# A two-layer decoder trunk: six experts fetched ahead and eleven groups instead of four and ten, and the second residual added by VectorE

## The chip, the cores and the metric

The kernel runs on one core of one Trainium2 chip. The metric is the device time of one execution in microseconds (us), as the median of three runs. TensorE (PE) multiplies matrices into the accumulation memory PSUM, VectorE (DVE) and ScalarE (ACT) do elementwise work, GpSimd (POOL) does a few small things, and SyncE (SP) issues nearly every DMA. Each engine works through its own instructions in program order and waits on semaphores for the others.

## The reference, cut to what matters

There are 256 tokens of width 1024 and two layers. A layer first mixes tokens (two kinds of attention, gated and projected), adds the residual and normalizes. Its second half is the part that the change touches:

```python
ffn = hierarchical_moe(x, ...)     # top-1 of 4 groups, then top-2 of 8 experts in that group: 32 experts of 1024 -> 256 -> 1024
ple = jax.nn.sigmoid(x @ w_ple_gate[i]) * (p[i] @ w_ple[i])
x = layer_norm(ALPHA * x + ffn + ple, ln2_g[i], ln2_b[i])
```

Each expert has 3 MB of f32 weights. All 32 are read in every layer, since all of them may be chosen by some token.

## The kernel before, in words

**Memory.** An arena of 47 places, each 128 partitions x 1024 f32 (512 KB), holds every weight tile and most long-lived tensors (class `Held`). A load takes the place that was freed longest ago and cannot start before the last reader of that place is done. All weight loads go through SP's queue in program order, so a load that waits for its place holds up those behind it.

**Experts.** Each expert has six weight tiles of one place: four (j = 0 to 3) for the gate and up projections and two (j = 4, 5) for the down projection. Experts are worked in groups that fill the 128 slots of a tile: two experts with 64 slots each, or four with 32. `groups` lists them: `npair` groups of two, the rest of four; `order` permutes them. The first `NFIX` experts are fixed by number, so that their loads need no routing result; the others are ranked by how many tokens chose them, the `NBIG` first ranks get 64 slots, and their ids are read by SP (`value_load`, L1034) when routing is done.

**The loop over groups** (`for gi in range(len(groups))`, PE in the written order): `front(gi + 1)` multiplies the gathered tokens of the next group with its j = 0 to 3 tiles in 32 strips of 32 slots, four strips side by side on the array; `back(gi)` does the down projection of the present group; then come the gathering of tokens for group gi + 2, the transposition of the hidden tile, `combine` (eight matmuls that add the group's output to the four accumulators `ya`), and the slot weights (`ways_of`). `front` frees its places as it goes, `back` its own at its end. At gi = 3 a branch (`leftover`) is tested, whose body is for an overfull expert.

**The input embedding** (class `Embed`, four quarters of 256 columns, two token tiles each): `products` multiplies into PSUM, `gate` takes the sigmoid (ACT) and the product (DVE) and splits it into a rounded part (ACT) and a rest (DVE), and `add` brings both into `ya` by two matmuls with the identity. Quarter 0 runs at gi = e1 = 2, the quarters 1 to 3 at the gi in `early`. In layer 0 the second token tile of quarter 3 runs after the loop.

**What stands ahead of the loop in SP's order:** the loads of the fixed experts, then of the embedding's quarters 1 to `nemb`, then (layer 0 only) `ahead`, four tiles of the next layer's first projection, which the loop splits at the gi in `pre_if`.

**The residual.** After the first norm, PE writes ALPHA * x into the accumulators with four f32 matmuls against a scaled identity (`residual`, tile `hT` in the trace): one ahead of the routing product of token tile 0, three behind that of token tile 1, while DVE works out the routing.

Of the kernel before, what the change touches and what calls it, by code (L numbers as in the profile page):

```python
# [11 lines left out]
F32 = mybir.dt.float32  # L12
# [5 lines left out]
OP = mybir.AluOpType  # L18
# [5 lines left out]
DEPTH = 2  # L24
P = 128
# [16 lines left out]
FAR = 1000.0  # L42


NFIX = 4
NBIG = 8


SEC = ["iq", "sq", "sk", "sv", "dq", "dk", "dv", "ga0", "ga1", "gb0", "gb1"]
# [30 lines left out]

@with_exitstack
def tile_hybrid_trunk(ctx: ExitStack, tc: tile.TileContext, x_in, xT_in, pT_in, pos_in, ws, wik, wrt, lnv,
                      brt, lamv, sublnv, out, places=47, t2b=4, young=4, gsb=1, hTb=1, silb=2, nring=5, early=(3, 4, 5), nahead=4, apart=8, npre=36, wA=1, wB=1, wC=1, wD=1, wE=3, inorder=2, e0=2, e1=2,  nearly_=0, peng_=1, ifat=3, im=0, df=0, dh=15, nol=0, diag=1, rpool='0000', lastemb=1, lastat=5, pre_if=(6,7), npair=4, fh=False, fg=0, order=(0,1,2,4,3,5,6,7,8,9), engs=None, nemb=3, nwarm=9, nfine=2, nah=4, o1=False, o2=False, o3=True, o4=True, order2=True, pa=2, pb=7, f1=True):
    nc = tc.nc
    V, A, G = nc.vector, nc.scalar, nc.gpsimd

# [40 lines left out]
    def wt(shape, dt, tag, bufs):  # L127
        return wk.tile(shape, dt, tag=tag, bufs=bufs, name=nm(tag))
# [33 lines left out]
    def load(l, i, shape):  # L162
        r = Held(shape, load=True)
        nc.sync.dma_start(r.t, ws[l, i])
        return r
# [19 lines left out]
    def t2(shape, dt=F32):  # L185
        return wt(shape, dt, "t2", t2b)
# [266 lines left out]
    for l in range(DEPTH):  # L453
# [278 lines left out]
        class Embed:  # L732
# [26 lines left out]
            def gate(self, t):  # L759
                b = self.b  # L760
                g = wt([P, 256], F32, "sil", silb)
                A.activation(g, b[:, :256], AF.Sigmoid)  # L762
                V.tensor_tensor(g, g, b[:, 256:], op=OP.mult)  # L763
                e = t2([P, 2, 256], F32R)
                split(e[:, 0, :], e[:, 1, :], g)
                self.e[t] = e
# [11 lines left out]
        xtT = [Held([4, S]) for _ in range(2)]  # L778
        logits = bank()
        ya = [[acc() for _ in range(2)] for _ in range(TT)]  # L780
        alphai = wt([P, 2 * P], F32, "hT", hTb)[:, :P]
        V.tensor_scalar(alphai, ident, ALPHA, None, op0=OP.mult)
        emb = {0: Embed(0)}

        def turn(t, h):
# [5 lines left out]
        def route(t, some=range(KT)):  # L791
            for k in some:
                PE.matmul(logits[:, t * 36:(t + 1) * 36], xtT[k // 4].v[:, k % 4, t * P:(t + 1) * P], wr36.v[:, k, :],
                          start=k == 0, stop=k == KT - 1)

        def residual(t, h):
            PE.matmul(ya[t][h], alphai, x[t].v[:, h * 512:(h + 1) * 512], start=True, stop=False)

        def normed(t, h):


            if t == 0:
                turn(t, h)
            elif h == 0:
                for f in (lambda: residual(0, 0), lambda: route(0), lambda: emb[0].products(0, range(0, wA)),
                          lambda: turn(1, 0)):
                    with in_turn():
                        f()
            else:
                for f in (lambda: emb[0].products(0, range(wA, wB)), lambda: turn(1, 1), lambda: route(1, range(4)),  # L810
                          lambda: emb[0].products(0, range(wB, wC)), lambda: route(1, range(4, KT)),
                          lambda: residual(0, 1), lambda: residual(1, 0), lambda: residual(1, 1)):
                    with in_turn():
                        f()
                if wD > wC:
                    with in_turn():
                        emb[0].products(0, range(wC, wD))
# [247 lines left out]
            split(*y, yp)  # L1065
            return y

        def combine(y, sT, h, t, stop=False):

            PE.matmul(ya[t][h], sT[:, t, :], y[0], start=False, stop=False)  # L1070
            PE.matmul(ya[t][h], sT[:, t, :], y[1], start=False, stop=stop)


# [41 lines left out]
                        fetch(r, j)  # L1115
        for q in range(1, 1 + nemb):
            emb[q] = Embed(q)
        if l < DEPTH - 1:
            ahead.extend(load(l + 1, i, [2, 512]) for i in range(KT // 2))

        def strips(gi):

# [80 lines left out]
        for gi in range(len(groups)):  # L1203
            if gi == ifat:
                most = nc.values_load(cmi[0:1, 0:1], min_val=0, max_val=S)
            here = lambda: tc.manual_schedule(engines={mybir.EngineType.PE})
            with here():
                after = front(gi + 1, *slots) if gi < last else None
            if gi == ifat:
                leftover(most)  # L1210
            with here():
                ys = back(gi, hT)
                if gi + 2 <= last:
                    marks, slots = marks_of(gi + 2), Gathered(gi + 2 >= fg)
                    for k4 in range(2):
                        gather(marks, slots.half[k4], k4)
                units = embeds(gi)
                for e, t, some in units[:1]:
                    e.products(t, some)
                if gi < last:  # L1220
                    hT = turned(after[0], wt([P, 2 * P], F32, "hT", hTb))
                    for h in range(2):
                        for t in range(TT):
                            combine(ys[h], sT, h, t)
                    sT = after[1]
                for e, t, _ in units[:1]:
                    e.gate(t)
                for e, t, some in units[1:]:
                    e.products(t, some)
                    e.gate(t)  # L1230
                if gi + 2 <= last:
                    slots = slots, *ways_of(gi + 2, marks)
                for e, t, _ in units:
                    e.add(t)
            if l < DEPTH - 1 and gi in pre_if:
                for r in ahead[:2] if gi == pre_if[0] else ahead[2:]:
                    ready.extend(parts(r.v[:, k, :]) for k in range(2))
                    r.free()
            if gi == last - 1:
                lng, lnb = wide(2, l), wide(3, l)  # L1240
                xn = [Held([D]) for _ in range(TT)]
                if l < DEPTH - 1:
                    xT = Split(KT)
# [12 lines left out]
        for t in range(TT):  # L1256
            if t == 1 and l < DEPTH - 1 and lastemb < 2:
                with behind(ends[0] if f1 else None):
                    emb[3].gate(1)
                emb[3].add(1)  # L1260
            for h in range(2):
                combine(ys[h], sT, h, t, True)
            if t == 0 and l < DEPTH - 1 and lastemb < 2:
                emb[3].products(1)
            with behind((ysplit[1] if o3 else None) if t == 0 else (copied[1] if order2 else None)):
                power = norm.stats(t)
            ends.append(power)
            ends[t:] = [norm.apply(t, o2)]
            powers.append(power)
# [70 lines left out]
```

## Time and profile before

| | us |
|---|---|
| median of three runs | 930.41 (929.46 to 930.71) |
| the profiled execution | 927.54 |
| its span, first to last instruction | 925.7 |
| PE busy in it | 890.5 (96%) |
| DVE, ACT busy | 423.5 (46%), 341.6 (37%) |
| DMA | 280.82 MB, mean 303 GB/s |

Positions below are us from the start of the span. The loop over expert groups runs from about 228 to 457 in layer 0 and from about 687 to 912 in layer 1. A busy PE in this profile includes matmuls that are slow to follow each other, so that 96% doesn't say that PE ends every wait: the starts of successive steps have to be compared.

### The profile page before, as it was taken

Reading aid. Unit: us, or ns where it says so; the run is one execution under the profiler, and the core shown is the slowest. Engines: PE = TensorE matmul, PEld = TensorE weight load, DVE = VectorE, ACT = ScalarE, POOL = GpSimd, SP = SyncE. Lnnn points to the kernel's source line nnn. Section 1 sums busy time; section 2 is a strip of 40 time slices with the busy share of each in tenths; the row PEclk is TensorE's granted clock in tenths of the full one; section 3 lists DMA queues with packets and bytes.
Section 4 is the critical chain, followed back from the end, with each engine's and each line's share of the span. In section 5 each row is a group of like instructions: output and inputs, shape, how many; then the busy total and the mean of one; then the engine's idle time right before and its main releaser. Section 6 shows DMA issues by size and latency. Waiting matters only on the chain. (4 is left out here: it accounts for less than half of the span.)

```text
span 925.7 us, 15402 instructions
## 1 busy us (share of the span) xinstructions
PE 890.5 (96%) x5473; PEld 588.0 (64%) x5473; DVE 423.5 (46%) x1064; ACT 341.6 (37%) x692; POOL 22.2 (2%) x29
## 2 busy tenths in 40 slices
PE   8999999999999999999999999999999998999994
PEld 5877677886466556543388777778865565556531
DVE  6797566776221121222368965677742211221214
ACT  6567677641121111221146565866321121111210
POOL 0000100000000000000100000000000000000010
PEclk9999999999999999999999999999999999999998
DMA  8995143866999999999998222448649999999993
GB/s 293 414 408 196 54 131 120 290 232 244 354 379 387 416 371 419 416 417 416 416 416 347 79 92 79 133 137 282 227 176 415 413 401 416 352 416 416 416 417 132
DMA packets 79011, 280.82 MB, mean 303 GB/s; under 512 B 9160, under 2 KB 9928, under 8 KB 78928
## 3 DMA queue, kind: packets, MB, share of 16 engines
q1 hardware_dynamic: 78784, 279.78, 78.3%
q8 instruction: 44, 0.72, 0.3%
q14 instruction: 39, 0.32, 0.1%
q10 hardware_dynamic: 144, 0.00, 0.0%
HBM read 278.70 MB, written 1.05 MB: 302 GB/s over the span
## 5 line engine op out<-in xcount | busy, mean ns | idle before, releaser
L92 PE MATMUL acc<-a,a 128*128 128x512 f32 x1440 | 352.0, 398 | 2.0 <-ACT a L208 1.2
L92 PEld LDWEIGHTS acc<-a,a 128*128 128x128 f32 x1440 | 265.5, 188 | 64.7 <-DVE a L209 3.2
L92 PE MATMUL mm<-a,a 128*32 128x512 f32 (+5 forms) x1648 | 229.2, 521 | 1.2 <-DMA a<-ws 1.1
L209 DVE TENSOR_TENSOR a<-a,a 128x512 fp32r<-128x512 f32 (+1 forms) x247 | 164.8, 688 | 50.8 <-ACT a L208 49.9
L208 ACT ACTIVATE a<-a 128x512 fp32r<-128x512 f32 (+1 forms) x247 | 151.1, 631 | 99.3 <-PE acc L92 69.7
L92 PEld LDWEIGHTS mm<-a,a 128*32 128x32 f32 (+3 forms) x1648 | 107.4, 132 | 96.9 <-issue 78.0
L92 PE MATMUL mm<-a,hT 128*32 128x512 f32 x640 | 102.9, 594 | 10.1 <-DMA a<-ws 5.3
L92 PEld LDWEIGHTS mm<-gs,a 128*128 128x128 f32 x640 | 73.1, 192 | 15.5 <-PE mm L92 10.9
L92 PE MATMUL mm<-gs,a 128*128 128x128 f32 x640 | 77.0, 278 | 0.0
L92 PEld LDWEIGHTS mm<-a,hT 128*32 128x32 f32 x640 | 24.2, 110 | 80.9 <-issue 48.0
L1051 DVE SCALAR_TENSOR_TENSOR sil<-sil,wsl,mm 128x256 f32<-128x256 f32 x20 | 9.6, 481 | 127.2 <-ACT sil L1050 127.0
L1050 ACT ACTIVATE sil<-mm 128x256 f32<-128x256 f32 x20 | 7.7, 384 | 160.8 <-PE mm L92 145.5
L209 DVE TENSOR_TENSOR t<-mm,t 128x512 fp32r<-128x512 f32 x40 | 27.6, 691 | 76.6 <-ACT t L208 76.6
L208 ACT ACTIVATE t<-mm 128x512 fp32r<-128x512 f32 x40 | 23.9, 597 | 86.5 <-PE mm L92 86.4
L919 DVE CAST sT<-mm 128x256 fp32r<-128x256 f32 x20 | 8.5, 425 | 84.7 <-PE mm L92 84.7
L92 PE MATMUL acc<-t,sT 128*128 128x512 f32 x160 | 43.8, 410 | 0.0
L906 ACT ACTIVATE a<-mm 128x512 f32<-128x512 f32 x36 | 21.5, 597 | 43.1 <-PE mm L92 41.7
L92 PEld LDWEIGHTS acc<-t,sT 128*128 128x128 f32 x160 | 28.3, 189 | 7.4 <-issue 1.7
L763 DVE TENSOR_TENSOR sil<-sil,mm 128x256 f32<-128x256 f32 x16 | 6.7, 417 | 54.4 <-ACT sil L762 54.4
L762 ACT ACTIVATE sil<-mm 128x256 f32<-128x256 f32 x16 | 6.1, 384 | 67.3 <-PE mm L92 67.3
L548 ACT ACTIVATE t<-mm,mx 128x128 f32<-128x128 f32 (+1 forms) x64 | 26.0, 421 | 11.5 <-DVE mx L545 11.5
L95 PE MATMUL mm<-identr,t 128*128 128x128 f32 (+1 forms) x132 | 21.8, 278 | 4.3 <-DVE t L581 4.3
(196 smaller groups left out, 614.6 us busy)
## 6 DMA issues: line engine op xcount, KB each, us to landing
a<-ws SPq DMA_DIRECT2D x523, 512.0 KB, 9.1
a<-x_in SPq DMA_DIRECT2D x2, 512.0 KB, 9.4
out<-a SPq DMA_DIRECT2D x4, 256.0 KB, 2.7
a<-xT_in SPq DMA_DIRECT2D x3, 256.0 KB, 6.7
a<-wik SPq DMA_DIRECT2D x2, 288.0 KB, 9.1
a<-ws SPq DMA_DIRECT2D x2, 256.0 KB, 3.0
pT<-pT_in SPq DMA_DIRECT2D x2, 256.0 KB
a<-wrt SPq DMA_DIRECT2D x2, 144.0 KB
```

The costliest lines, as they stand in the source:

```text
L92: self.last = nc.tensor.matmul(*a, **k)
L95: self.last = nc.tensor.transpose(*a, **k)
L208: copied[0] = A.activation(hi, src, AF.Copy)
L209: copied[1] = eng.tensor_tensor(lo, src, hi, op=OP.subtract)
L548: A.activation(e[:, i * nk:(i + 1) * nk], b[:, i * nk:(i + 1) * nk], AF.Exp, bias=mx[:, i:i + 1], accum_out=sums[i])
L762: A.activation(g, b[:, :256], AF.Sigmoid)
L763: V.tensor_tensor(g, g, b[:, 256:], op=OP.mult)
L906: A.activation(xg, b.rearrange("p (k s) -> p k s", k=4), AF.Copy)
L919: V.tensor_copy(sT, b[:, :2 * P].rearrange("p (t q) -> p t q", t=TT))
L1050: A.activation(sil, gu[:, :FE], AF.Sigmoid)
L1051: V.scalar_tensor_tensor(sil, sil, wsl, gu[:, :FE], op0=OP.mult, op1=OP.mult)
```

## The change

Four constants of the plan move (the signature line is left out of the diff): `NFIX` 4 to 6, `NBIG` 8 to 12, `npair` 4 to 6, so that there are six groups of two and five of four, eleven in all, in the order (0,1,2,6,3,7,4,8,5,9,10). Of the embedding, quarter 1 alone is loaded ahead (`nemb` 3 to 1); `early` goes from (3,4,5) to (4,5,6), `lastat` from 5 to 6, `pre_if` from (6,7) to (7,8). The `ahead` loads move into the loop, to gi = 5. The residual's matmuls and the scaled identity go; instead DVE adds ALPHA * x to the gated embedding, and the first group's `combine` starts the accumulation.

```diff
-NFIX = 4
-NBIG = 8
+NFIX = 6
+NBIG = 12
...
                 V.tensor_tensor(g, g, b[:, 256:], op=OP.mult)
+                V.scalar_tensor_tensor(g, x[t].v[:, self.q * 256:(self.q + 1) * 256], ALPHA, g, op0=OP.mult, op1=OP.add)
                 e = t2([P, 2, 256], F32R)
...
-        alphai = wt([P, 2 * P], F32, "hT", hTb)[:, :P]
-        V.tensor_scalar(alphai, ident, ALPHA, None, op0=OP.mult)
...
-        def residual(t, h):
-            PE.matmul(ya[t][h], alphai, x[t].v[:, h * 512:(h + 1) * 512], start=True, stop=False)
...
-        if l < DEPTH - 1:
-            ahead.extend(load(l + 1, i, [2, 512]) for i in range(KT // 2))
...
-                            combine(ys[h], sT, h, t)
+                            combine(ys[h], sT, h, t, start=gi == 0)
...
+            if l < DEPTH - 1 and gi == pre_if[0] - 2:
+                ahead.extend(load(l + 1, i, [2, 512]) for i in range(KT // 2))
```

**SP, layer 0, the end of what is issued ahead of the routing result.** L164 is a load of the embedding or of the next layer, L1040 (after: L1035) one of an expert, TENSOR_LOAD of `ids` the first read of a ranked expert's number. Before:

```order
L164 DMA a_452_2295<-ws 128x1024
L164 DMA a_453_2297<-ws 128x1024
L164 DMA a_454_2299<-ws 128x1024
L164 DMA a_455_2301<-ws 128x1024
L164 DMA a_456_2303<-ws 128x1024
L164 DMA a_457_2305<-ws 128x1024
L1034 TENSOR_LOAD ids_420_2224
```

After:

```order
L1035 DMA a_452_2291<-ws 128x1024
L1035 DMA a_453_2293<-ws 128x1024
L1035 DMA a_454_2295<-ws 128x1024
L1035 DMA a_455_2297<-ws 128x1024
L1035 DMA a_456_2299<-ws 128x1024
L164 DMA a_459_2305<-ws 128x1024
L1029 TENSOR_LOAD ids_419_2218
```

Expert tiles stand where tiles of the embedding and of the next layer stood.

**PE, layer 0, from the routing product of token tile 1 to the first matmul on the routing mask.** `hT` is the scaled identity, the 128x36 rows are the routing product. Before:

```order
L92 MATMUL mm_393_2071<-a_361_1901,a_392_2070 128x36 x4
L92 MATMUL acc_395_2073<-a_277_1487,hT_398_2076 128x512
L92 MATMUL acc_396_2074<-a_278_1488,hT_398_2076 128x512
L92 MATMUL acc_397_2075<-a_278_1488,hT_398_2076 128x512
L92 LDWEIGHTS onesb_111
```

After:

```order
L95 MATMUL mm_408_2135<-identr_108,a_278_1488 128x128 x4
L92 MATMUL mm_393_2071<-a_361_1901,a_391_2069 128x36 x4
L92 MATMUL mm_393_2071<-a_361_1901,a_392_2070 128x36 x4
L92 LDWEIGHTS onesb_111
L92 MATMUL mm_412_2173<-t2_409_2149,onesb_111 32x32
```

Nothing is left on PE between the routing product and the mask.

**PE, layer 0, where the second unit of an embedding quarter is added** (`acc<-t2,identr`), among the strips of the next group's front. Before:

```order
L92 MATMUL mm_644_3332<-a_628_3273,a_614_3177 32x512
L92 MATMUL acc_396_2074<-t2_624_3242,identr_108 128x256 x2
L92 MATMUL mm_644_3332<-a_629_3284,a_614_3177 32x512
L92 MATMUL mm_644_3332<-a_630_3295,a_614_3177 32x512
L92 MATMUL mm_644_3332<-a_631_3306,a_614_3177 32x512
```

After:

```order
L92 MATMUL mm_663_3451<-a_655_3426,a_641_3330 32x512
L92 MATMUL acc_396_2074<-t2_651_3397,identr_108 128x256
L92 MATMUL mm_663_3451<-a_655_3426,a_641_3330 32x512
L92 MATMUL mm_663_3451<-a_656_3437,a_641_3330 32x512 x2
L92 MATMUL mm_663_3451<-a_657_3439,a_641_3330 32x512
L92 MATMUL acc_396_2074<-t2_651_3397,identr_108 128x256
```

Five strips stand ahead of the first add in both; the second add now follows four strips later.

## Rows read from the trace of the kernel before

**Rows 1.** PE in order of time, a back of layer 1: start, busy us, line, operation.
```profile
727.57 3.62 PE L92 MATMUL mm<-a,hT 128*32 128x512 f32 x32
```

**Rows 2.** ACT in order of time, layer 1: the sigmoid that follows each front.
```profile
856.17 0.38 ACT L1050 ACTIVATE sil<-mm 128x256 f32<-128x256 f32 x1 [7.68 <-PE mm L92]
872.99 0.39 ACT L1050 ACTIVATE sil<-mm 128x256 f32<-128x256 f32 x1 [8.88 <-PE mm L92]
890.66 0.38 ACT L1050 ACTIVATE sil<-mm 128x256 f32<-128x256 f32 x1 [9.70 <-PE mm L92]
```

**Rows 3.** PE in order of time, the last two backs of layer 1.
```profile
890.05 1.02 PE L92 MATMUL mm<-a,hT 128*32 128x512 f32 x2
...
901.48 0.44 PE L95 MATMUL mm<-identr,sil 128*128 128x128 f32 x2
...
903.86 1.65 PE L92 MATMUL mm<-a,hT 128*32 128x512 f32 x8
...
909.41 2.76 PE L92 MATMUL mm<-a,hT 128*32 128x512 f32 x18 [0.17 <-DMA a<-ws]
912.10 2.22 PE L92 MATMUL acc<-t,sT 128*128 128x512 f32 x8
```

**Rows 4.** ACT in order of time, layer 0: the sigmoids of the last two fronts.
```profile
407.21 0.39 ACT L1050 ACTIVATE sil<-mm 128x256 f32<-128x256 f32 x1 [8.88 <-PE mm L92]
...
436.13 0.38 ACT L1050 ACTIVATE sil<-mm 128x256 f32<-128x256 f32 x1 [14.69 <-PE mm L92]
```

**Rows 5.** PE in order of time, the last two backs of layer 0.
```profile
435.52 2.20 PE L92 MATMUL mm<-a,hT 128*32 128x512 f32 x4
...
446.81 0.44 PE L95 MATMUL mm<-identr,sil 128*128 128x128 f32 x2
...
449.18 1.06 PE L92 MATMUL mm<-a,hT 128*32 128x512 f32 x8
...
456.94 0.73 PE L92 MATMUL acc<-t,sT 128*128 128x512 f32 x2
```

**Rows 6.** Windows: start:end, length, busy us (count) of PE, PEld, DVE, ACT, POOL, PEclk, DMA share, GB/s.
```profile
225.00:230.00 5.00, 4.84 (x42) 3.04 (x45) 3.19 (x22) 1.39 (x4) 0.00 (x0) 1.00 0.01 3
245.00:250.00 5.00, 5.00 (x49) 1.74 (x51) 1.07 (x4) 0.44 (x1) 0.00 (x0) 1.00 0.71 260
325.00:350.00 25.00, 25.00 (x179) 15.25 (x178) 5.17 (x14) 4.65 (x10) 0.00 (x0) 1.00 0.99 375
400.00:425.00 25.00, 23.92 (x165) 10.20 (x168) 6.99 (x20) 5.12 (x10) 0.00 (x0) 1.00 1.03 417
680.00:685.00 5.00, 4.61 (x24) 2.54 (x24) 4.08 (x30) 1.16 (x6) 0.00 (x0) 1.00 0.00 0
685.00:690.00 5.00, 4.84 (x50) 2.24 (x48) 1.84 (x13) 0.90 (x2) 0.00 (x0) 1.00 0.26 84
```

**Rows 7.** PE in order of time, layer 1, around the routing.
```profile
673.35 1.02 PE L92 MATMUL acc<-a,hT 128*128 128x512 f32 x2
...
676.66 1.29 PE L95 MATMUL mm<-identr,a 128*128 128x128 f32 x8
677.98 1.98 PE L92 MATMUL mm<-a,a 128*128 128x36 f32 x16
679.79 2.82 PE L92 MATMUL acc<-a,hT 128*128 128x512 f32 x6
683.00 0.21 PE L92 MATMUL mm<-t,onesb 128*32 128x32 bf16 x2 [0.39 <-DVE t L862]
```

**Rows 8.** DVE in order of time, the last step of the first norm, layer 1.
```profile
675.77 1.41 DVE L414 SCALAR_TENSOR_TENSOR a<-a,rs,a 128x512 f32<-128x512 f32 x2
```

**Rows 9.** Windows with PE idle: in the branch of layer 0, and after the last matmul.
```profile
312.00:314.00 2.00, 0.00 (x0) 0.00 (x0) 0.90 (x2) 0.38 (x1) 0.00 (x0) 1.00 1.03 422
917.40:917.60 0.20, 0.00 (x0) 0.00 (x0) 0.20 (x2) 0.00 (x0) 0.00 (x0) 0.61 0.00 0
```

**Rows 10.** Page, costliest groups: DVE's three-operand form on a 128x256 tile.
```profile
L1051 DVE SCALAR_TENSOR_TENSOR sil<-sil,wsl,mm 128x256 f32<-128x256 f32 x20 | 9.6, 481 | 127.2 <-ACT sil L1050 127.0
```

More of the change, by code (lines that the diff above doesn't have):

```diff
@@ L82, in tile_hybrid_trunk @@
 def tile_hybrid_trunk(ctx: ExitStack, tc: tile.TileContext, x_in, xT_in, pT_in, pos_in, ws, wik, wrt, lnv,
-                      brt, lamv, sublnv, out, places=47, t2b=4, young=4, gsb=1, hTb=1, silb=2, nring=5, early=(3, 4, 5), nahead=4, apart=8, npre=36, wA=1, wB=1, wC=1, wD=1, wE=3, inorder=2, e0=2, e1=2,  nearly_=0, peng_=1, ifat=3, im=0, df=0, dh=15, nol=0, diag=1, rpool='0000', lastemb=1, lastat=5, pre_if=(6,7), npair=4, fh=False, fg=0, order=(0,1,2,4,3,5,6,7,8,9), engs=None, nemb=3, nwarm=9, nfine=2, nah=4, o1=False, o2=False, o3=True, o4=True, order2=True, pa=2, pb=7, f1=True):
+                      brt, lamv, sublnv, out, places=47, t2b=4, young=4, gsb=1, hTb=1, silb=2, nring=5, early=(4, 5, 6), nahead=4, apart=8, npre=36, wA=1, wB=1, wC=1, wD=1, wE=3, inorder=2, e0=2, e1=2,  nearly_=0, peng_=1, ifat=3, im=0, df=0, dh=15, nol=0, diag=1, rpool='0000', lastemb=1, lastat=6, pre_if=(7,8), npair=6, fh=False, fg=0, order=(0,1,2,6,3,7,4,8,5,9,10), engs=None, nemb=1, nwarm=9, nfine=2, nah=4, o1=False, o2=False, o3=True, o4=True, order2=True, pa=2, pb=7, f1=True):
     nc = tc.nc
@@ L804, in normed @@
             elif h == 0:
-                for f in (lambda: residual(0, 0), lambda: route(0), lambda: emb[0].products(0, range(0, wA)),
+                for f in (lambda: route(0), lambda: emb[0].products(0, range(0, wA)),
                           lambda: turn(1, 0)):
@@ L810, in normed @@
                 for f in (lambda: emb[0].products(0, range(wA, wB)), lambda: turn(1, 1), lambda: route(1, range(4)),
-                          lambda: emb[0].products(0, range(wB, wC)), lambda: route(1, range(4, KT)),
-                          lambda: residual(0, 1), lambda: residual(1, 0), lambda: residual(1, 1)):
+                          lambda: emb[0].products(0, range(wB, wC)), lambda: route(1, range(4, KT))):
                     with in_turn():
@@ L1066, in halves_of, with combine @@
             return y
-        def combine(y, sT, h, t, stop=False):
-            PE.matmul(ya[t][h], sT[:, t, :], y[0], start=False, stop=False)
+        def combine(y, sT, h, t, start=False, stop=False):
+            PE.matmul(ya[t][h], sT[:, t, :], y[0], start=start, stop=False)
             PE.matmul(ya[t][h], sT[:, t, :], y[1], start=False, stop=stop)
@@ L1261, in tile_hybrid_trunk @@
             for h in range(2):
-                combine(ys[h], sT, h, t, True)
+                combine(ys[h], sT, h, t, stop=True)
             if t == 0 and l < DEPTH - 1 and lastemb < 2:
```

## The prediction, made before the run

> **What bounds the kernel now.** I read the windows first, then PE's order of time through both loops over groups, then the sigmoids that close each front, since their distances show a group's whole period. The reader is to see three things.
>
> First, the loop is paced by two engines in turn. In its middle PE runs without a wait: from one sigmoid to the next without an embedding, 872.99 - 856.17 = 16.82 us [rows 2], for groups of two and of four alike, because a front always has 32 strips and a back 16. Towards the end it waits for weights. An expert tile of 512 KB at 417 GB/s [rows 6] takes 1.26 us, so a group of four (24 tiles) takes 30.2 us to load and a group of two 15.1, against PE's 16.82.
>
> Second, these waits can be added up. An undisturbed back takes 3.6 us [rows 1]. In layer 1 the last front comes 17.67 us after the one before it (0.85 too long) [rows 2], and the last two backs take 901.48 - 890.05 = 11.43 and 912.10 - 903.86 = 8.24 us [rows 3], 7.8 and 4.6 too long: 13.3 us in all. In layer 0 the last front comes 28.92 us after its predecessor, 12.1 too long [rows 4], and the backs take 11.29 and 7.76 [rows 5], 7.7 and 4.2 too long: 24.0 us.
>
> Third, the DMA engines stand still between the last tile that needs no routing result and the first that does: they move 3 GB/s from 225 to 230, nothing from 680 to 685 and 84 GB/s up to 690 [rows 6]. Before this stretch they have brought 24 expert tiles, 7 of the embedding and, in layer 0 alone, 4 of the next layer.
>
> **The change part by part.** All times are against the profiled execution, 927.54 us, of which the span is 925.7; the median of the runs shown is 2.87 higher, and I carry the difference that I find over to the median.
>
> *One more group.* Each layer gets an eleventh group, 16.82 us of PE. PE does it with the same strips, so nothing of it is cheaper for having two experts in it.
>
> *Six experts ahead.* At the routing result 36 expert tiles and 2 of the embedding are there: 38, where there were 35 in layer 0 and 31 in layer 1. What is left to load up to the last expert tile is 156 expert tiles, 5 of the embedding and in layer 0 the 4 `ahead`, that is 165 and 161 against 168 in both. The DMA's end can come 3 x 1.26 = 3.8 us earlier in layer 0 and 7 x 1.26 = 8.8 us in layer 1. The new tiles go into the stretch where the DMA stands still, which costs nothing there.
>
> *Layer 1.* The DMA wait of 13.3 us would have to be given back by DMA that ends only 8.8 us earlier, but PE itself also comes later: with no wait at all its last back begins at 903.86 - (0.85 + 7.8) + 16.82 = 912.0, and the last tile, which came about 909.4 [rows 3], would now come about 901. PE therefore finds all weights there and sets the end: -13.3 + 16.8 = **+3.5 us**.
>
> *Layer 0.* By PE alone it would be -24.0 + 16.8 = -7.2 us. By DMA alone it is -3.8. The DMA is the later of the two, so the end moves by **-3.8 us**, and its bounds are -7.2 and, if nothing of the three tiles is kept, 0.
>
> Whether they are kept depends on places. When the ids arrive, 47 less x (2), its transpose (2), quarter 0 (3) and the prefetched tiles leave 5 places in layer 0 before and 2 after. Before, the DMA already runs out of places once PE is between two fronts: 260 GB/s from 245 to 250 [rows 6], (1 - 260/417) x 5 = 1.9 us lost. With 3 places fewer this stall grows by 3.8 us. But a second stall should go: from 325 to 350 the rate is 375, 2.5 us lost [rows 6], because an embedding stood beside gi = 3 and held PE back while places were short. With the embedding moved on by one group, PE frees the places of that group of four earlier by the length of an embedding. The stalls roughly cancel; I keep -3.8.
>
> *The residual on PE.* Removed are eight instructions per layer, 1.02 + 2.82 us [rows 7]. The three matmuls behind the routing product lie beside DVE's routing arithmetic, which PE waits for anyway (until 683.00). The one ahead of it ends sooner, but the transposes that follow (676.66) need DVE's half of the norm that ends at 675.77 + 0.7 = 676.5 [rows 8], so at most 0.2 us. The bounds are -1.0 and 0 per layer; I take 0.
>
> *The residual on DVE.* Eight three-operand instructions per layer at 0.48 us [rows 10], 3.9 us on an engine that is mostly idle in the loop. For the first unit of a quarter, the products of the second cover it on PE. For the second, the sum lies between the sigmoid and PE's adds, which stand among the strips of the next front. Counted in passes of four strips, five strips, add, four, add and 23 are as many as five, both adds and 27. A wait of up to 0.48 is possible in each; layer 1 has four such places, so 0 to 1.9 us. I take 0.1 each: +0.4 us. In layer 0 the DMA covers it. At the end of layer 0 one such sum stands ahead of the second half of the norm, with the next layer's matmuls beside it: 0 to 0.5, taken as +0.2.
>
> *Loads moved within SP's order.* The quarters 2 and 3 and `ahead` are now issued in the loop. Behind them stand expert tiles, ahead of PE by more than a group at that point; the 9 tiles in layer 0 and 5 in layer 1 are already in the counts above. Nothing further.
>
> The sum: +3.5 + 0.4 - 3.8 + 0.2 = **+0.3 us**, so 930.41 + 0.3 = 930.7. What this kernel's measurement can tell from no change is about 0.2%, 1.9 us.
>
> **The rivals.**
>
> *The clock falls in the routing gap (slower).* Without its three matmuls PE has nothing from 679.8 to 683.0 [rows 7], 3.2 us. In this trace PE kept the granted clock of 1.00 (2.4 GHz) through 2 us of idleness at 312 to 314, but after its last matmul (912.10 + 2.22 = 914.3) the clock was halved (1.2 GHz) by 917.5 [rows 3, 9], also 3.2 us. The gap is on the edge. The price: until the clock is back, what PE does from 683.0 on takes twice as long; no row here shows matmuls at the lower clock, so between 0 and the 7 us up to 690, of which PE is busy nearly all [rows 6], per layer; with nothing nearer I take half of that, 3.5. The chain from the routing to the first front is PE's in both layers, so nothing hides it: 934 with one layer hit, 938 with both. Against it: only the gap's length speaks for it, and there is work right before and after. The Trainium skill, "TensorE: Matmul & The Clock Gate", in "Why this matters for your kernels", advises against long idle gaps between bursts of matmuls since they bring the lower clock back; by that rule both layers would be hit, and the time would be 938. The trace agrees with it only at its end.
>
> *The prefetch finds no room (slower).* If the second stall of layer 0 stays while the first grows, the 3.8 us are lost: layer 0 at 0, layer 1 at +3.5 and the small terms make +4.1, 934.5. This is the case in which the change doesn't do what it says, since the extra expert merely takes the place of other tiles. For it speaks that only 2 places are free; against it, that the DMA's late stall coincides with the embedding that moves.
>
> *PE sets the end of layer 0 too (faster).* If the DMA loses less than I think in its stalls, layer 0 gets up to -7.2, and the sum is -7.2 + 3.5 + 0.2 = -3.5: 926.9. The stalls seen in the first 120 us of the loop leave room for it, the 3.4 us by which the DMA is later in my sum speak against it.
>
> **How the numbers follow.** My forecast has 0.50, the clock 0.20, no room 0.15, PE in both layers 0.15. The forecast's own range is 928.9 to 932.6 (0.1 to 0.5 us on each of the small terms, 1.5 on the stalls). Beyond it the range takes in the faster case in part and the slower ones up to one fallen clock with a lost prefetch: 927.5 to 935.5. Faster: 0.13 from the faster case and 0.02 from the forecast. Slower: 0.20 from the clock, 0.11 from no room, 0.04 from the forecast. The rest, 0.50, is no change.
>
> **What would show it.** Right: in layer 1 no wait for weights in the last backs and eleven sigmoids, about 16.8 us apart where there is no embedding, the last back's end 3 to 5 us later in the loop's own time; in layer 0 the DMA busy between 225 and 228, the last back still waiting for tiles, its end about 4 us earlier. Wrong: PE waits for weights at the end of layer 1, a DMA gap before the routing result as long as now, a granted clock under 1.00 near 222 to 232 or 680 to 692, or PE standing still at the adds of the embedding.

## The result, and the profile after

The changed kernel takes 939.56 us (937.5 to 942.5, four executions), the kernel before 929.93 us measured beside it: the ratio is 1.0102 [1.0082, 1.0121]. The change is slower by about 1%; I had forecast 930.7, and the time lies above the range too. The profiled execution of after has a span of 935.6 us against 925.7. Two executions far from all others, one of e10_moved at 1258.5 us and one of the kernel before beside it at 2305.6, are left out of every comparison below.

**The clock.** The view by cores gives the span and TensorE's mean granted clock, which was 0.996 in the kernel before:

```profile
core 0: 935.6 us, clock 0.988
```

PE in order of time, layer 1 of after, around the routing (start, busy us, line, operation; in brackets the idle time before it and what ended it); the answer to [rows 7]:

```profile
679.05 1.29 PE L95 MATMUL mm<-identr,a 128*128 128x128 f32 x8 [0.41 <-DVE a L414]
680.37 1.98 PE L92 MATMUL mm<-a,a 128*128 128x36 f32 x16
685.39 0.23 PE L92 MATMUL mm<-t,onesb 128*32 128x32 bf16 x2 [3.05 <-DVE t L857]
...
685.69 2.05 PE L92 MATMUL mm<-a,a 128*128 128x256 f32 x4
687.53 3.54 PE L92 MATMUL mm<-gs,a 128*128 128x128 f32 x16
```

The last two of these in the kernel before, and from ACT's rows its first sigmoid of layer 1:

```profile
683.27 1.11 PE L92 MATMUL mm<-a,a 128*128 128x256 f32 x4
684.22 2.02 PE L92 MATMUL mm<-gs,a 128*128 128x128 f32 x16
...
697.86 0.38 ACT L1050 ACTIVATE sil<-mm 128x256 f32<-128x256 f32 x1 [3.38 <-PE mm L92]
```

The windows of after over that stretch (columns as in [rows 6]):

```profile
682.00:683.00 1.00, 0.34 (x4) 0.23 (x3) 0.58 (x6) 0.01 (x1) 0.00 (x0) 1.00 1.00 410
683.00:684.00 1.00, 0.00 (x0) 0.00 (x0) 0.88 (x6) 0.66 (x4) 0.00 (x0) 1.00 1.06 434
684.00:685.00 1.00, 0.00 (x0) 0.00 (x0) 0.88 (x8) 0.00 (x0) 0.00 (x0) 0.52 1.01 414
685.00:690.00 5.00, 4.61 (x23) 4.24 (x24) 2.80 (x18) 0.49 (x2) 0.00 (x0) 0.50 0.33 133
```

The reader is to see the chain. Where three residual matmuls stood, PE waits 3.05 us for DVE. The granted clock falls from 1.00 (2.4 GHz) to 0.50 (1.2 GHz) at about 684, while PE is idle, and stays there past 690. The products of the embedding then take 2.05 us instead of the 1.11 of the same four matmuls before, the gathering 3.54 instead of 2.02. Layer 0 shows the same (2.05 and 3.20 us, clock 0.50 from 224 to 230). From the first matmul on the mask to the first front's sigmoid it was 14.86 us in both layers of the kernel before; now it is 16.97 and 17.31: +2.11 and +2.45 us.

**The loops.** ACT in order of time, layer 1 of after, the sigmoids of the first front, of two around an embedding and of the last two (the answer to [rows 2]):

```profile
702.70 0.38 ACT L1045 ACTIVATE sil<-mm 128x256 f32<-128x256 f32 x1 [3.38 <-PE mm L92]
...
796.32 0.39 ACT L1045 ACTIVATE sil<-mm 128x256 f32<-128x256 f32 x1 [8.88 <-PE mm L92]
...
823.89 0.38 ACT L1045 ACTIVATE sil<-mm 128x256 f32<-128x256 f32 x1 [7.30 <-PE mm L92]
...
895.77 0.39 ACT L1045 ACTIVATE sil<-mm 128x256 f32<-128x256 f32 x1 [8.80 <-PE mm L92]
...
912.62 0.38 ACT L1045 ACTIVATE sil<-mm 128x256 f32<-128x256 f32 x1 [8.80 <-PE mm L92]
```

PE in order of time, the end of both loops of after (the answer to [rows 3, 5]):

```profile
454.72 1.04 PE L92 MATMUL mm<-a,hT 128*32 128x512 f32 x2 [0.23 <-DMA a<-ws]
455.99 2.76 PE L92 MATMUL mm<-a,hT 128*32 128x512 f32 x18 [0.22 <-DMA a<-ws]
458.68 0.74 PE L92 MATMUL acc<-t,sT 128*128 128x512 f32 x2
...
912.37 3.62 PE L92 MATMUL mm<-a,hT 128*32 128x512 f32 x32
...
918.33 3.64 PE L92 MATMUL mm<-a,hT 128*32 128x512 f32 x32
921.90 2.25 PE L92 MATMUL acc<-t,sT 128*128 128x512 f32 x8
```

In layer 1 the last two fronts are 16.85 us apart and both last backs take 3.6 us: no wait for weights is left, PE sets the end. In layer 0 the last back still waits for tiles.

**Where the 9.9 us of the spans went.** Before against after, stretch by stretch, each between the starts of two rows of PE or ACT (the end of a back is taken as the start of the row behind it):

| stretch | before | after | difference |
|---|---|---|---|
| start to the mask matmuls, layer 0 | 224.46 | 225.32 | +0.86 |
| mask to the first sigmoid, layer 0 | 14.86 | 16.97 | +2.11 |
| first sigmoid to the end of the last back, layer 0 | 217.62 | 216.39 | -1.23 |
| from there to the mask matmuls, layer 1 | 226.06 | 226.71 | +0.65 |
| mask to the first sigmoid, layer 1 | 14.86 | 17.31 | +2.45 |
| first sigmoid to the last back's end, layer 1 | 214.24 | 219.20 | +4.96 |
| the rest | 13.60 | 13.70 | +0.10 |

My sum had -3.8, +0.2 and +3.9 in the third, fourth and sixth row and nothing in the others. These are single executions: a second profile of after (e13 below) has +0.13 in the third row and +2.45, +2.02 and +5.07 in the second, fifth and sixth.

### The profile page after: what moved, and what is told of

Read it like the earlier page. It is cut to its first block, busy times and chain, and to the rows that moved or that the text cites. A ratio compares the mean times of both kernels' runs of the same rounds, so it can differ in the third digit from the quotient of the medians.

```text
span 935.6 us, 15941 instructions
## 1 busy us (share of the span) xinstructions
PE 898.3 (96%) x5745; PEld 604.4 (65%) x5745; DVE 436.8 (47%) x1090; ACT 348.0 (37%) x704; POOL 22.4 (2%) x29
## 5 line engine op out<-in xcount | busy, mean ns | idle before, releaser
L92 PE MATMUL mm<-a,a 128*32 128x512 f32 (+5 forms) x1776 | 241.1, 528 | 0.5 <-ACT a L788 0.5
L92 PEld LDWEIGHTS mm<-a,a 128*32 128x32 f32 (+3 forms) x1776 | 110.8, 131 | 96.2 <-issue 80.6
L92 PEld LDWEIGHTS mm<-gs,a 128*128 128x128 f32 x704 | 83.7, 198 | 17.1 <-PE mm L92 12.6
L92 PE MATMUL mm<-a,hT 128*32 128x512 f32 x704 | 88.2, 593 | 5.7 <-DMA a<-ws 5.2
L92 PE MATMUL mm<-gs,a 128*128 128x128 f32 x704 | 87.4, 284 | 0.0
L209 DVE TENSOR_TENSOR t<-mm,t 128x512 fp32r<-128x512 f32 x44 | 30.4, 691 | 53.9 <-ACT t L208 53.9
L208 ACT ACTIVATE t<-mm 128x512 fp32r<-128x512 f32 x44 | 26.3, 597 | 64.8 <-PE mm L92 64.8
L92 PE MATMUL acc<-t,sT 128*128 128x512 f32 x176 | 48.2, 410 | 0.0
L901 ACT ACTIVATE a<-mm 128x512 f32<-128x512 f32 x40 | 23.9, 598 | 49.1 <-PE mm L92 49.1
L92 PEld LDWEIGHTS acc<-t,sT 128*128 128x128 f32 x176 | 31.2, 189 | 8.1 <-DVE t L209 1.0
```

Of the source, the lines that this page charges most:

```text
L92: self.last = nc.tensor.matmul(*a, **k)
L208: copied[0] = A.activation(hi, src, AF.Copy)
L209: copied[1] = eng.tensor_tensor(lo, src, hi, op=OP.subtract)
L901: A.activation(xg, b.rearrange("p (k s) -> p k s", k=4), AF.Copy)
```

## Experiments

The theory: what was wrong is the price of nothing for the residual on PE; the clock falls (the first rival). Against it: the lateness at the head of the loop is swallowed by later waits, and the eleven groups cost the time; or VectorE's sum delays the adds.

**Work put back that nobody needs (e1_fill).** The changed kernel with the four matmuls at their old places; the first group's `combine` overwrites what they give.

```diff
...
+        def residual(t, h):
+            PE.matmul(ya[t][h], alphai, x[t].v[:, h * 512:(h + 1) * 512], start=True, stop=True)
...
-                for f in (lambda: route(0), ...
+                for f in (lambda: residual(0, 0), lambda: route(0), ...
...
-                          ... lambda: route(1, range(4, KT))):
+                          ... lambda: route(1, range(4, KT)),
+                          lambda: residual(0, 1), lambda: residual(1, 0), lambda: residual(1, 1)):
```

> The changed kernel, with the four matmuls of the residual put back on PE at their old places as work whose result is thrown away (the first group's combine starts the accumulators anew). Theory 'gap' (without them PE stands idle for 3.05 us while DVE works out the routing, the granted clock is halved, and PE's work up to the first front takes longer: 2.1 us in layer 0 and 2.45 us in layer 1 by the traces): the clock stays at 1.00 in both stretches, and the time is about 939.6 - 4.6 = 935.0 us. Rival 'plan' (the lateness at the head of the loop would be swallowed by later waits for weights, and the whole 9.6 us come from the eleven groups): 939.6 us or, with the added work, up to 0.5 us more, whatever the clock does. Rival 'DVE' (the sum on VectorE delays the adds): no change either, 939.6.

Measured: 932.2 us, ratio to before 1.0037 [1.0023, 1.0051]. Sixteen matmul instructions more in all, and 7.4 us less (by the two ratios, 0.65%, 6 us). Windows of this kernel, both routing stretches:

```profile
220.00:230.00 10.00, 9.45 (x70) 5.72 (x73) 5.93 (x42) 2.06 (x8) 0.00 (x0) 1.00 0.57 227
680.00:690.00 10.00, 9.45 (x71) 4.72 (x69) 5.78 (x42) 2.06 (x8) 0.00 (x0) 1.00 0.52 205
```

The clock stays at 1.00. "Gap" is right, though its 4.6 us were too few; both rivals had no change at all and are out. What VectorE's sum costs beside the clock is read from e3 below.

**The residual alone on VectorE (e2_resdve).** The kernel before with ten groups and four ahead, the residual as in the changed kernel.

```diff
+                V.scalar_tensor_tensor(g, x[t].v[:, self.q * 256:(self.q + 1) * 256], ALPHA, g, op0=OP.mult, op1=OP.add)
...
-            PE.matmul(ya[t][h], alphai, x[t].v[:, h * 512:(h + 1) * 512], start=True, stop=False)
...
+                            combine(ys[h], sT, h, t, start=gi == 0)
```

> The kernel before, with the residual alone moved from PE to VectorE; ten groups, four experts ahead, everything else as before. Theory 'gap': the clock falls after the routing as in the changed kernel, +2.1 and +2.45 us, and they are not swallowed, since the loads that end the loop start only when the ids are read, which comes later by the same amount; with 0.65 us at the end of layer 0 and adds that the waits for weights cover: about 930 + 5.2 = 935 us. Rival 'plan': 930 to 931 us. Rival 'DVE' (the adds wait, 0.35 us for each embedding of two units): up to 932.

Measured: 935.44 us (932.66 to 938.71), 1.0062 [1.0041, 1.0083]; as "gap" expected. Its profile (937.9 us, mean clock 0.984, of which a part is a fall to 0.68 from 10 to 15 us) shows something more. PE in order of time, layer 1:

```profile
681.19 2.49 PE L92 MATMUL mm<-a,a 128*128 128x36 f32 x18 [0.25 <-ACT a L788]
684.08 1.82 PE L95 MATMUL mm<-identr,a 128*128 128x128 f32 x8 [0.40 <-DVE a L414]
685.73 3.63 PE L92 MATMUL mm<-a,a 128*128 128x36 f32 x16
692.40 0.24 PE L92 MATMUL mm<-t,onesb 128*32 128x32 bf16 x2 [3.04 <-DVE t L857]
```

and its windows there:

```profile
682.00:684.00 2.00, 1.68 (x13) 1.27 (x12) 2.00 (x4) 0.00 (x0) 0.98 (x1) 1.00 1.02 412
684.00:685.00 1.00, 0.92 (x5) 0.88 (x6) 0.59 (x1) 0.00 (x0) 0.00 (x0) 0.61 0.63 254
685.00:690.00 5.00, 4.35 (x21) 3.98 (x19) 0.57 (x6) 1.19 (x2) 0.00 (x0) 0.50 0.04 11
690.00:697.00 7.00, 4.60 (x23) 4.23 (x24) 4.56 (x31) 1.16 (x6) 0.00 (x0) 0.50 0.00 1
```

The clock falls at about 684.4, before the routing gap, where the fourth residual matmul used to stand between the transposes and the first routing product. The last routing product takes 3.63 us instead of 1.98, and the gap then keeps the clock down until 697. From the first routing product to the first sigmoid (709.72) it is 28.53 us here, 26.54 in layer 1 of after. So there may be two places.

**The plan alone (e3_plan), and eleven groups alone (e4_eleven).** The first has the changed kernel's six ahead, eleven groups and moved loads with the residual on PE as before; the second only the eleven groups.

```diff
 e3_plan, against the changed kernel
-                V.scalar_tensor_tensor(g, x[t].v[:, self.q * 256:(self.q + 1) * 256], ALPHA, g, op0=OP.mult, op1=OP.add)
...
+            PE.matmul(ya[t][h], alphai, x[t].v[:, h * 512:(h + 1) * 512], start=True, stop=False)
...
 e4_eleven, against the kernel before
-NBIG = 8
+NBIG = 12
-... early=(3, 4, 5), lastat=5, pre_if=(6,7), npair=4, order=(0,1,2,4,3,5,6,7,8,9)
+... early=(4, 5, 6), lastat=6, pre_if=(7,8), npair=6, order=(0,1,2,6,3,7,4,8,5,9,10)
```

> The plan of the changed kernel alone: six experts ahead, eleven groups and the moved loads, with the residual on PE as before. Theory 'gap': the change less the clock (4.6), the end of layer 0 (0.65) and the slower embeddings of layer 1 (about 1.1): 939.6 - 6.3 = 933.3 us, that is still 3 us above before, so the plan is itself worse than the +0.3 less 0.6 that I had predicted for it. If my sum for the plan holds and something else costs the rest: 929.7. Rival 'plan': 939 us.

> The kernel before with eleven groups (12 experts of 64 slots, 20 of 32) but four experts ahead, the embedding's three quarters and the next layer's loads ahead as before, the residual on PE. My sum for it: layer 1 +3.5 us by PE (its weights are there without any further prefetch, the last tile at about 909.4 against a last back that begins at 912), layer 0 unmoved by the DMA: 933.4 us. Theory 'six ahead is worth nothing here': the same time as the whole plan (six ahead) within 0.5 us. Theory 'six ahead shortens the DMA by 3.8 us in layer 0': the plan is 3.8 us faster than this.

Measured: the plan 929.66 us, 1.0005 [0.9994, 1.0016]; eleven groups alone 928.49, 0.9992 [0.9981, 1.0003]. The plan costs nothing by the medians, which is what my sum without the DVE terms (-0.3) had said, and takes 3.6 us less than I expected here; e4 takes 4.9 less than the 933.4 expected. By the profiled spans the two are 1.6 and 1.3 us longer than before (927.3 and 927.0 against 925.7). Medians and spans aren't reconciled here. Six ahead bring nothing on top: from the first sigmoid to the last back's end, layer 0 takes 216.96 us with them and 216.50 without, layer 1 216.40 and 216.30. Windows of e3_plan, where the three tiles are lost again:

```profile
231.00:260.00 29.00, 27.27 (x243) 16.25 (x236) 6.04 (x18) 6.86 (x12) 0.00 (x0) 1.00 0.89 310
325.00:350.00 25.00, 25.00 (x186) 16.54 (x179) 4.08 (x10) 4.27 (x10) 0.00 (x0) 1.00 1.02 416
```

and of e4_eleven:

```profile
231.00:260.00 29.00, 27.26 (x245) 16.00 (x238) 6.05 (x18) 6.45 (x11) 0.00 (x0) 1.00 0.95 362
325.00:350.00 25.00, 25.00 (x186) 16.54 (x181) 4.06 (x10) 4.24 (x9) 0.00 (x0) 1.00 1.03 417
```

(417 - 310) / 417 x 29 = 7.4 us are lost between 231 and 260 with six ahead, 3.8 without: the difference, 3.6, is the three tiles. The later stall (375 GB/s before [rows 6]) goes in both, by the eleven groups.

E1 less the plan, 932.2 - 929.66 = 2.5 us, is VectorE's part (1.7 by the two spans, 929.0 and 927.3).

**Which of the matmuls (e6_gap, e7_front).** As e1_fill, but with only the three in the routing gap, or only the one ahead of the first routing product.

```diff
 e6_gap, against e1_fill
-                for f in (lambda: residual(0, 0), lambda: route(0), ...
+                for f in (lambda: route(0), ...
 e7_front, against e1_fill
-                          lambda: residual(0, 1), lambda: residual(1, 0), lambda: residual(1, 1)):
```

> The changed kernel with three of the four residual matmuls put back as work that is thrown away, those behind the last routing product; nothing ahead of the first routing product. Theory 'two places' (the clock falls in the routing gap in every execution, 4.6 us over both layers, and in some executions already in the norm, where the fourth matmul stood, some 2 to 3 us more): the gap stays at 1.00, about 932.2 us + what the norm costs by itself, 933 to 935, with a granted clock under 1.00 around 218 or 675 in some executions. Rival 'the gap alone' (with the gap filled the norm's short waits never bring the clock down): 932.2 us, as with all four.

> The changed kernel with only the one residual matmul ahead of the first routing product put back as work that is thrown away; the routing gap stays empty. Theory 'two places': the clock falls in the routing gap in both layers, but no earlier: 932.2 + 4.6 = 936.8 us, and the granted clock of all executions near 0.988. Rival 'the gap alone': as the changed kernel, 939.6 us, with executions at 0.982 among them.

Measured: e6_gap 935.94 us, two executions at 930.8 and 931.6 with a mean clock of 0.995, five at 935.2 to 939.9 with 0.986 to 0.991. e7_front 936.22 us, all six executions at 0.988 to 0.991. Against e1 they lose 0.36% and 0.45% by the ratios, where the changed kernel loses 0.65%: each half alone leaves more than half of the loss. "Two places" is supported, with the place in the norm so far seen once.

**The one matmul moved, nothing left out (e10_moved).** The kernel before, with the matmul ahead of the first routing product moved to the other three.

```diff
-                for f in (lambda: residual(0, 0), lambda: route(0), ...
+                for f in (lambda: route(0), ...
...
-                          lambda: residual(0, 1), ...
+                          lambda: residual(0, 0), lambda: residual(0, 1), ...
```

> The kernel before with one residual matmul moved: the one ahead of the first routing product now stands with the other three behind the last; nothing is left out and PE has work in the routing gap. Theory 'two places' (the matmul ahead of the first routing product also keeps the clock up, in the norm's short waits, which fall only in some executions): 931 to 935 us with a wide spread, executions with a granted clock under 0.992 among them, and where the profiled one is among these, a PEclk under 1.00 that begins before the last routing product. Rival 'the gap alone': 929.8 us (the moved matmul lies beside DVE's routing work in both places, 0.5 us at most), all clocks at 0.993 to 0.996.

Measured: 1.0028 [1.0003, 1.0052]. Of twelve executions six took 927.2 to 931.7 us at a clock of 0.993 or more, six 934.3 to 938.5 at 0.985 to 0.991; the kernel before, beside it, took 928.2 to 932.5. That is the wide spread that "two places" expected, without a profile of it. So seven more executions were profiled: of e6_gap (e11, e14, e15), of e10_moved (e12, e16, e17) and of the changed kernel (e13). The edits are those above.

> The changed kernel with the routing gap filled by three thrown-away matmuls once more, for one more profile. Theory 'two places': if this execution's mean granted clock is under 0.993, PEclk falls below 1.00 in the stretch of the norm (216 to 224 or 674 to 684), before the gap. Rival: it falls elsewhere, in the branch at 312 or in the first 20 us, as the kernel before does in some of its executions.

> The kernel before with the one residual matmul moved behind the last routing product, for a profile of it. Theory 'two places': if this execution's mean granted clock is 0.991 or lower, PEclk falls below 1.00 between the first routing product and the first matmul on the mask (216 to 224, or 674 to 683), and that layer's first front comes 1.5 to 4 us later than in the kernel before. Rival: in such an execution it falls in the first 20 us or in the branch.

> The changed kernel once more, for a second profile of it. Theory 'two places': its granted clock is near 0.982 to 0.984, and in at least one layer PEclk falls before the last routing product is done, so that the product itself takes longer than its 1.98 us and the head of that layer's loop comes later than the 2.1 to 2.45 us of the first profile. Rival: in both layers it falls only in the routing gap, and where the mean clock is lower, another fall stands in the first 20 us or in the branch near 315.

> The changed kernel with the routing gap filled by three thrown-away matmuls, for another profile. Theory 'two places': if the mean granted clock is under 0.992, PEclk falls below 1.00 in the norm (216 to 224 or 674 to 684). Rival: it falls in the first 20 us or in the branch near 315.

> The changed kernel with the routing gap filled by three thrown-away matmuls. Theory 'two places': if its mean granted clock is under 0.992, PEclk falls below 1.00 between the first routing product and the mask (216 to 224 or 674 to 684). Rival: it falls in the first 20 us or in the branch.

> The kernel before with one residual matmul moved behind the last routing product. Theory 'two places': if its mean granted clock is under 0.992, PEclk falls below 1.00 between the first routing product and the mask, and the head of that layer's loop comes 1.5 to 4 us later. Rival: it falls in the first 20 us or in the branch.

> The same kernel as the look before it (one residual matmul moved behind the last routing product), another execution, with the same two expectations: a fall between the first routing product and the mask where the mean clock is under 0.992, or, by the rival, in the first 20 us or in the branch.

Measured: e11 930.79 us (0.995), e12 928.57 (0.995), e14 933.79 (0.996), without a fall in the norm; e11 has one after the branch, at 315 to 320. e13, the changed kernel, 938.54 (0.989): it falls in the routing gap of both layers, as in the first profile (+2.45 and +2.02 us from the mask to the first sigmoid), and not in the norm; there the rival was right. e15 937.01 (0.991), e16 934.16 (0.991) and e17 938.71 (0.984) have it in the norm, e15 and e16 in layer 0, e17 in both. PE in order of time, layer 0 of e15_gap_look:

```profile
214.75 2.49 PE L92 MATMUL mm<-a,a 128*128 128x36 f32 x18 [0.25 <-ACT a L790]
217.65 1.94 PE L95 MATMUL mm<-identr,a 128*128 128x128 f32 x8 [0.41 <-DVE a L414]
219.42 3.63 PE L92 MATMUL mm<-a,a 128*128 128x36 f32 x16
222.85 5.26 PE L92 MATMUL acc<-a,hT 128*128 128x512 f32 x6
228.05 0.21 PE L92 MATMUL mm<-t,onesb 128*32 128x32 bf16 x2
```

and its windows:

```profile
215.00:220.00 5.00, 4.59 (x29) 3.98 (x28) 3.09 (x7) 1.16 (x3) 0.98 (x1) 0.75 1.03 416
220.00:225.00 5.00, 5.00 (x18) 3.97 (x18) 1.71 (x14) 0.89 (x5) 0.00 (x0) 0.50 0.96 391
225.00:230.00 5.00, 5.00 (x21) 2.38 (x21) 2.32 (x17) 0.49 (x2) 0.00 (x0) 0.72 0.00 2
```

Here even the filling work takes 5.26 us instead of 2.82. From the first routing product to the first sigmoid it is 28.17 us (242.92), and 24.10 in layer 1 of e14, where the clock stays: +4.1. In e17 it is 29.01 and 29.08 against 24.49 and 24.50 in e12, the same kernel with the clock at 1.00: +4.5 and +4.6, a little more than the 1.5 to 4 expected. "Two places" is shown for kernels that lack the one matmul. In the changed kernel both profiles have the gap alone; that its executions at 0.982 to 0.984 fell in the norm as well is inferred, not seen.

**Towards something better (e5_five, e8_order, e9_five_order).** Ten groups with five ahead; ten groups in another order; both.

```diff
 e5_five
-NFIX = 4
+NFIX = 5
...
-        if l < DEPTH - 1:
+            if l < DEPTH - 1 and gi == pre_if[0] - 2:
                 ahead.extend(load(l + 1, i, [2, 512]) for i in range(KT // 2))
 e8_order
-... order=(0,1,2,4,3,5,6,7,8,9)
+... order=(0,1,4,2,5,3,6,7,8,9)
 e9_five_order: both
```

> The kernel before with five experts ahead and still ten groups (8 experts of 64 slots), the next layer's loads moved into the loop, three quarters of the embedding ahead, the residual on PE. 37 tiles are there at the routing result instead of 35 and 31. If tiles fetched ahead shorten the loads' end: layer 0 -2.5 us, layer 1 -7.6 us (of 13.3 us of waits), 920 us. If the places are what bounds (six ahead gave nothing in layer 0: the eleven groups with four and with six ahead took the same time within 1.2 us): 929 to 930 us, with the rate of the loads between 231 and 260 and between 691 and 730 falling by what was gained.

> The kernel before with another order of its ten groups: groups of four at the third and fifth place (0,1,4,2,5,3,6,...) instead of the fourth and sixth. If the loads are held up early in the loop because groups of two free too few places (8.0 us lost to rates under 417 GB/s between 245 and 350 in layer 0, 4.9 between 690 and 820 in layer 1), a group of four earlier frees them sooner: -3 to -6 us in layer 0 and -2 to -4 in layer 1, 921 to 925 us. If PE must then wait for the 24 tiles of the earlier group of four, the gain is lost: 930 us or more.

> The kernel before with both: five experts ahead (ten groups, the next layer's loads moved into the loop) and the order with groups of four at the third and fifth place. If a group of four that frees 16 places in its front gives the further tiles their room: up to -2.5 us in layer 0 and -7.6 us in layer 1 below the new order alone (923.2), 913 to 921 us. If the room is short before that group's front (231 to 260, where five ahead alone moved 349 and 314 GB/s against 385 and 348 before), the tiles fetched ahead are lost there as before: 922 to 924 us.

Measured: five ahead 928.6 us, 0.9990 [0.9976, 1.0003], no gain; the order 923.22, 0.9935 [0.9915, 0.9955]; both 921.21, 0.9902 [0.9879, 0.9925]. The last two beat both kernels, with the same work as before. Windows of e8_order, where the kernel before moved 382 GB/s (280 to 300) and 375 [rows 6], and in layer 1 402 and 370:

```profile
280.00:300.00 20.00, 20.00 (x153) 12.32 (x146) 3.23 (x7) 3.85 (x8) 0.00 (x0) 1.00 1.03 417
325.00:350.00 25.00, 25.00 (x180) 15.22 (x179) 4.87 (x12) 4.65 (x10) 0.00 (x0) 1.00 1.03 416
730.00:760.00 30.00, 30.00 (x224) 20.58 (x226) 4.99 (x13) 5.71 (x12) 0.00 (x0) 1.00 1.03 416
790.00:820.00 30.00, 30.00 (x207) 18.37 (x206) 6.92 (x20) 5.39 (x12) 0.00 (x0) 1.00 1.03 419
```

A group of four frees 16 places in one front and 24 in all, a group of two half of that in the same time; put earlier, the loads no longer run out of places after 280. From the first sigmoid to the last back's end layer 0 takes 215.29 us instead of 217.62, layer 1 212.25 instead of 214.24, each a little less than expected. With five ahead as well layer 1 takes 209.71, 2.5 less. But 1.3 of that goes with a stop of PE behind the branch (last section), longer in e8's profile (0.66 us) than in e9's (0.24): the group there takes 30.99 us and 29.70. So some 1.2 are left of the 7.6 hoped for; between 690 and 730 the rate is 323 GB/s (406 with the order alone). Whether e9 is faster than e8 is not settled: the intervals overlap.

## Why the prediction was wrong, step by step

**The step that failed** is "The residual on PE": "The bounds are -1.0 and 0 per layer; I take 0." Those matmuls lay beside DVE's routing work, as I said, and cost no time: from the transposes ahead of them to the mask it is 10.52 us before (672.48 to 683.00) and 10.51 after (674.88 to 685.39). But they did something: they kept PE busy while it waits for VectorE, and with it the clock. The price of taking them away, by the runs: 2.0 to 2.5 us in each layer where the clock falls in the routing gap (both layers in both profiles of the changed kernel; 1.4 and 1.8 in e7), about 2 us more where it falls already in the norm (layer 1 of e2: 28.53 against 26.54), together 7.4 us in the medians, 6 by the ratios (e1). I had this as a rival with a chance of 0.20 and 3.5 us a layer. Its chance was far too low, and its sum was about right by luck: the gap costs less than 3.5, and the rest comes from a place that the rival didn't name. I had looked at the gap behind the last routing product only. The matmul ahead of the first I called shorter by "at most 0.2 us" and did not ask what stands around it.

The rule that I had weighed (the Trainium skill, "TensorE: Matmul & The Clock Gate", in "Why this matters for your kernels") warns of idle gaps between bursts of matmuls. For the routing gap, 3.05 us, the traces now agree with it in both layers. That warning doesn't cover the norm: there PE waited 0.25 and 0.41 us only, among transposes and narrow products, and the clock fell in three of the seven profiles with the gap filled and the one matmul missing (e6, e11, e12, e14 to e17). Of the 19 timed executions of e6 and e10, 11 have a mean clock of 0.991 or less.

**Layer 1, +3.5 for the group and the waits: right.** Measured +4.96, of which the embedding is 4 x 0.35 (below); 3.56 are left. The mechanism is as described, no wait in the last backs. Before and after both have the stop of PE behind the branch (last section); the plan alone hasn't, and its 216.40 us are 2.16 more than before, but 3.35 more than the 213.05 of e5, which has ten groups and a stop of 0.23 us only.

**Layer 0, -3.8: wrong in size**, -1.23 and +0.13 in the two profiles of the changed kernel, -0.66 in the plan alone. The stall after 231 grew by 3.6 us as priced, and the later stall went (416 instead of 375 GB/s), but that gain is the eleven groups' own, as e4 shows; it doesn't give the tiles their room. "The stalls roughly cancel" counted it for the prefetch. This is the second rival, "no room". The medians don't bear it out: with layer 0 at nothing the plan alone would be some 3.5 us over the kernel before, and it took 929.66 against 929.83. So the size of this term stays open.

**VectorE's sum, +0.4 in the loop: right in place, wrong in size and mechanism.** The adds don't wait: in the profile no wait stands ahead of them. They cost because the second is split off from the first. PE in order of time, layer 1, after:

```profile
816.76 0.39 PE L92 MATMUL acc<-t,identr 128*128 128x256 f32 x1
817.08 1.06 PE L92 MATMUL mm<-a,a 128*32 128x512 f32 x8
818.08 0.39 PE L92 MATMUL acc<-t,identr 128*128 128x256 f32 x1
818.39 4.92 PE L92 MATMUL mm<-a,a 128*32 128x512 f32 x43
```

and the same place in e3_plan:

```profile
809.50 0.50 PE L92 MATMUL acc<-t,identr 128*128 128x256 f32 x2
809.93 5.78 PE L92 MATMUL mm<-a,a 128*32 128x512 f32 x51
```

Two single adds are 0.78 instead of 0.50 us, and strips that run four side by side are broken off once more. The period of this group goes from 27.22 us (816.28 - 789.06 in e3) to 27.57 (823.89 - 796.32 in after), +0.35, and layer 1 has four such places. The Trainium skill, "TensorEngine Tiling (Array Packing)", "Key Properties", says that changing the tiling mode drains TensorE; that fits a matmul over the whole array between strips of a quarter, and I had not used it. The rest of the 2.5 us of the medians isn't assigned: 1.24 stands in layer 1's loop by the spans of e1 and e3, 0.2 in layer 0's.

**The end of layer 0, +0.2:** +0.65 measured, of which the plan alone already has 0.46 (226.52 us in e3 against 226.06). VectorE's sum is left with 0.2.

**What is chance in the +9.9.** The +0.86 ahead of the first routing: e1 and e3, which load the same tiles and run the same up to there, reach the mask at 224.22 and 224.00, and the changed kernel itself does at 224.96 in e13.

## What to carry to other kernels

Work on PE that lies beside a wait isn't free to remove: look at all the stretches that it fills, give the fall of the clock a price and a chance of its own there, and keep the work if that is dearer, even if nobody needs its result. Prefetching deeper pays only if there is room behind it; where a loop is paced by places, ask first which order of the same work frees them sooner. A median hides a cost that falls in half of the executions: compare the mean clock of each execution, and profile until both kinds are seen.

## What the runs showed of the hardware

The same program's clock falls or doesn't, from one execution to the next, at more than one place: in the norm (above), and after the branch at gi = 3 of layer 0, where PE waits 2 us (PEclk 0.66 from 315 to 320 in e5, e7 and e11, 1.00 in before, in after and in e14, the same kernel as e11). There it costs 1.7 us: the group behind the branch takes 31.24 us in e5 against 29.54 in before, 20.84 in e7 against 19.14 in after. In e2 and e9 it also falls within the first 20 us (0.66 from 10 to 20 in e9).

Behind the same branch, in layer 1, PE stops once more in some executions for nothing that the profile shows. PE in order of time, layer 1, after:

```profile
777.58 3.63 PE L92 MATMUL mm<-a,hT 128*32 128x512 f32 x29 [1.87 <-DMA a<-ws]
781.71 1.05 PE L92 MATMUL mm<-a,hT 128*32 128x512 f32 x3 [0.51 <-issue]
```

Before and e8 have it as well (0.71 and 0.66 us), e14 and e15 with 1.38, e5 and e9 with 0.23 and 0.24, e1 to e4 not: the next sigmoid is 20.47 us after the branch's in after, 18.92 in e1. It is 1.55 us that no edit explains, since e6 and e14 are the same kernel and only e14 has it (21.32 against 18.93). The Trainium skill, "Runtime: NRT & Kernel Launch", "Instruction fetch mechanics", says that a taken branch breaks the sequential fetch of instructions and can stall the engine. That would fit; no run here separates it from other causes.
